# Between two expert mixtures: moving averages as banded products, and a new order of the stage

## The chip, the cores and the metric

The kernel runs on one core of a Trainium2 chip. The metric is the device time of one execution in microseconds; of several executions the median is given. All engines of the core work at the same time: PE (TensorE; PEld is its weight load), DVE (VectorE), ACT (ScalarE), POOL (GpSimd) and SP (SyncE, which here issues the weight transfers). Each works through its own instructions in order and waits at an instruction until what it needs is there. Results of PE go to PSUM, which the kernel divides into eight banks of 128 x 512 numbers of 32 bits; DVE and ACT take them from there.

## What is computed

A two-layer model over 512 tokens of width 1024. Layer 0 is attention, layer 1 averages over neighbouring tokens; each is followed by a mixture of 32 experts with two chosen per token. The stage at issue lies between the two mixtures:

```python
mod_l = (cond_lat @ w_ada[i] + b_ada[i])[:, None, :]
sh_m, sc_m, g_m, sh_f, sc_f, g_f = jnp.split(mod_l, 6, axis=-1)
h_l = modulate(rms_norm(x_lat, norm_mix_g[i]), sh_m, sc_m)       # h * (1 + scale) + shift
...
for gi, win in enumerate((2, 4, 8, 16)):                         # pool_mixer: 4 groups of 256 columns
    lo = jnp.maximum(t - win // 2, 0)
    hi = jnp.minimum(t + win // 2, n)
    mean = (cg[:, hi] - cg[:, lo]) / (hi - lo)                   # cg: running sum over the tokens
    outs.append((mean - h[..., sl]) @ w_pool[gi])
...
x_lat = x_lat + g_m * o_l
tokens = modulate(rms_norm(x_lat, norm_ffn_g[i]), sh_f, sc_f)
f = hierarchical_moe(tokens, ...)                                # group by argmax, then the two best experts
```

## The kernel before

All of x stays on chip as four tiles of 128 tokens by 1024 columns (`self.x(j)`, j = 0 to 3). Weights arrive as tiles of 1 MiB through one stream: `Stream` (L115) issues the loads on SP in a fixed order, at most 12 tiles are resident at a time, and `st.done()` after the last use of a tile lets the next load be issued. Tiles of this size, the weights among them, share 22 slots (`big`, L516).

**The mixture** (`moe`, L1547) runs 16 pairs of experts: up product, activation, down product, scatter back. The last pair of the first mixture is written out in `last_down` (L1416): the down product in two halves of the columns, `parted` (the gated rows, split into a high and a low part by DVE, ACT, DVE), `added` (scatter on PE, addition to x on DVE, squares on ACT), and then the norms `r` of the four token tiles. In the stream, eight tiles of `w_ada` follow the last expert of the first mixture, and behind them come the twelve tiles of the first pair of the second mixture. At the start of a mixture, `overflow` (L1479) makes every engine, SP too, read a count from DVE (`fullest`); only then does SP issue further loads.

**The stage between** (`pool_layer`, L1649) does this:
- `ada` (L1654): the modulation vectors of layer 1's mixture from `w_ada`, eight steps of four products each on PE (`ada_part`, L351); at the end `ada_rows` is copied by DVE, and `ada_end` (L432) turns the rows on PE and adds biases on DVE.
- `scaled` (L1638): x times its norm, token tiles 0 and 2 on DVE, 1 on ACT, 3 on POOL.
- `turned(k)` (L1663): for each of the eight column blocks k, four transposes on PE (tokens along the free axis), then scale and shift on ACT into a padded buffer.
- `sums(k)` (L1677): the moving sum by repeated doubling, one addition for a window of 2, up to four for a window of 16, and two small corrections at the edges; for k = 7, 5 and 3 on POOL, else on DVE. `less(k)` (L1691): mean minus input, on DVE. Group g consists of k = 2g and 2g + 1 and has the window 2, 4, 8 or 16.
- `project(g)` (L1698): eight products on PE; `added(g)` (L1712): addition to x on DVE and squares on ACT.
- `router` (L1120): 16 products on PE, then DVE scales the router weights. `turn(k)` (L1723) transposes x for the router, `logits` (L1732) are 16 products for four k. Norm (`rstd_of`), `norm_high` on ACT and `norm_low` on DVE make a high and a low part of the scaled tokens; `add_shift`, `choose` and `rank` on DVE choose the experts; `zeros` (L1323) clears four PSUM banks by a product of zeros; `gather_part` (L1329) gathers the tokens of the first eight experts by 64 products, and the second mixture begins.

The order on every engine is the order in which the program issues the instructions; there is no planner. It stands at the end of `pool_layer`: `turned` for 7, 0, 1, 6, 5; two ada steps; sums; `project(0)`, and so on, with `project(3)`, `project(2)`, `project(1)`, `ada_end` and `router` in this order.

Of the kernel before, what the change touches and what calls it, by code (L numbers as in the profile page):

```python
# [60 lines left out]

_C = {}
_off = 0
for _n, _w in (("ident", 128), ("iota", SEQ), ("tcol", NT), ("w8", EPG), ("w4", NG),
               ("islot", UNIT), ("edge", 4 * 16), ("tri", 128), ("cos", NT * HD), ("sin", NT * HD)):
    _C[_n] = (_off, _off + _w)
    _off += _w
# [3 lines left out]
def make_consts():  # L71
# [25 lines left out]
    sn = np.stack([-sn, sn], axis=-1).reshape(NT, 128, HD).transpose(1, 0, 2)  # L97
    put("cos", cs.reshape(128, -1))
# [84 lines left out]
class Kernel:  # L183
# [3 lines left out]
    def build(self):  # L187
        tc, nc, a = self.tc, self.nc, self.a
        with ExitStack() as es:
# [12 lines left out]
            with ExitStack() as sm:  # L202
# [7 lines left out]
                norms = self.moe(0, self.prepare_pool(), xe, later=later)  # L210
# [1112 lines left out]
    def zeros(self, k, tag):  # L1323
# [92 lines left out]
    def last_down(self, aT, w, gf, inv, after):  # L1416
# [38 lines left out]
        products(1, 1)  # L1455
        parted(1)
# [90 lines left out]
    def moe(self, i, late, first, then=lambda: None, later=iter(())):  # L1547
# [41 lines left out]
        for p in range(NPAIR):  # L1589
# [22 lines left out]
            if p == NPAIR - 1:  # L1612

                nc.scalar.activation(self.sm.tile([128, 1], F32, name="warm", bufs=1), self.rk[:, 0, 0:1], AF.Sqrt)
                return self.last_down(aT, w, gf, inv, then)
# [22 lines left out]
    def scaled(self, norms, outs):  # L1638

        nc = self.nc  # L1640
        engs = nc.vector, None, nc.vector, nc.gpsimd
        for j, r in norms:
            if engs[j] is None:
                nc.scalar.activation(outs[j], self.x(j), AF.Copy, scale=r)
            else:
                engs[j].tensor_scalar(outs[j], self.x(j), r, 0.0, op0=ALU.mult, op1=ALU.add)

    def pool_layer(self, norms):
        nc, mp, pm, st, sm, pw = self.nc, self.mp, self.pm, self.st, self.sm, self.pw  # L1649
        xn = [self.big([128, 2, D], F32, "xn") for _ in range(2)]  # L1650
        xnj = [xn[j // 2][:, j % 2] for j in range(NT)]
        self.ada_begin(pm, 1, 2, "ga")

        def ada(n):  # L1654
            for _ in range(4 * n):
                self.ada_part()

        ada(1)
        self.scaled(norms, xnj)
        PAD = 16  # L1660
        A, B = self.AB[1, 1, 0], self.AB[1, 0, 0]

        def turned(k):  # L1663

            ab = self.big([128, 3, SEQ + 2 * PAD], F32, "pab")
            h = ab[:, 0]
            nc.gpsimd.memset(h[:, :PAD], 0.0)
            nc.gpsimd.memset(h[:, PAD + SEQ:], 0.0)
            p = pm.tile([128, 512], F32, tag=("y", "c")[k // 2 % 2], name="pt")
            for j in range(NT):  # L1670
                nc.tensor.transpose(p[:, j * 128:(j + 1) * 128], xnj[j][:, k * 128:(k + 1) * 128], self.ident)
# [228 lines left out]
```

## Time and profile before

| | |
|---|---|
| time, median of 3 runs | 1384.36 us (1382.53 to 1388.68) |
| time of the profiled execution | 1387.86 us |
| its span | 1386.1 us |
| busy share of the span | PE 95%, DVE 48%, ACT 26%, POOL 11% |
| moved by DMA | 475.49 MB, mean 343 GB/s |

All times in the rows are microseconds from the start of the span. The first mixture ends at about 843, the stage between lasts until 911.5, the second mixture from there to 1362. In the page's forty slices, the moved GB/s are at 415 to 427 in both mixtures and fall to 130 and 266 in the two slices that hold the stage between. A busy PE is not a PE at its peak: a product is shown until its result is there, so the distance between starts is the price of one in a series.

### The profile page before, as it was taken

To read this page: it belongs to the slowest core of one execution; us is meant where nothing else is said; L and a number is where in the kernel's file an instruction comes from. 1 tells how busy PE (TensorE), PEld (TensorE's weight loads), DVE (VectorE), ACT (ScalarE), POOL (GpSimd) and SP (SyncE) were. 2 spreads that over 40 slices of the span, in tenths; PEclk is the share of its full clock that TensorE was granted. 3 is DMA by queue.
4 is the path that set the end of the run, shared out by engine and by line. 5 is a ranking of instruction groups with operands and counts; after the bars stand their busy time and mean duration, and the time that the engine had idled before them with its cause. 6 is when DMAs were issued, how large, how long until landed. Compare 5 with 4: busy or idle time off the path is not lost. (4 is left out here: it accounts for less than half of the span.)

```text
span 1386.1 us, 18610 instructions
## 1 busy us (share of the span) xinstructions
PE 1315.6 (95%) x7139; PEld 735.6 (53%) x7139; DVE 669.5 (48%) x1296; ACT 362.1 (26%) x703; POOL 146.4 (11%) x154
## 2 busy tenths in 40 slices
PE   4799999999899999999999997899999999999995
PEld 1578677778645444454444434654445444454442
DVE  2778788867824343343433437743334342343325
ACT  2554687763311111111111114421111111111103
POOL 1523343340000000000000014000000000000001
PEclk8799999999999999999999999999999999999998
DMA  9411836159489999999999999369999999999994
GB/s 374 166 62 61 342 143 215 52 187 389 191 368 427 427 427 426 426 427 426 427 426 427 422 417 416 130 266 396 427 427 426 427 426 427 426 426 427 426 421 172
DMA packets 80561, 475.49 MB, mean 343 GB/s; under 512 B 8497, under 2 KB 10049, under 8 KB 30289
## 3 DMA queue, kind: packets, MB, share of 16 engines
q1 hardware_dynamic: 80456, 474.22, 83.3%
q8 instruction: 58, 0.95, 0.3%
q14 instruction: 39, 0.31, 0.1%
q10 hardware_dynamic: 8, 0.01, 0.0%
HBM read 472.09 MB, written 2.11 MB: 342 GB/s over the span
## 5 line engine op out<-in xcount | busy, mean ns | idle before, releaser
L1356 PE MATMUL pgate<-wt,xe 128*64 128x512 f32 x1024 | 271.3, 593 | 2.8 <-ACTq L1488 2.2
L1356 PE MATMUL pup<-wt,xe 128*64 128x512 f32 x1024 | 270.2, 592 | 0.3 <-DVEq L1488 0.3
L1381 PE MATMUL py<-wt,aT 128*64 128x512 f32 x960 | 212.6, 595 | 0.0
L1361 DVE TENSOR_TENSOR act<-act,pup 128x512 f32<-128x512 f32 x32 | 22.0, 688 | 341.8 <-ACT act L1360 309.6
L1412 DVE TENSOR_TENSOR x<-x,pc 128x512 f32<-128x512 f32 x240 | 154.1, 684 | 29.8 <-PE pc L1410 29.8
L1356 PEld LDWEIGHTS pgate<-wt,xe 128*64 128x64 f32 x1024 | 75.6, 137 | 147.5 <-issue 129.8
L1356 PEld LDWEIGHTS pup<-wt,xe 128*64 128x64 f32 x1024 | 76.5, 137 | 145.2 <-issue 142.8
L1410 PE MATMUL pc<-y,scat 128*128 128x512 f32 x480 | 136.6, 406 | 2.4 <-DVE x L1412 2.4
L1394 DVE SCALAR_TENSOR_TENSOR py<-py,r_sw,gw 128x512 f32<-128x512 f32 x64 | 48.6, 759 | 178.4 <-PE py L1381 169.4
L1381 PEld LDWEIGHTS py<-wt,aT 128*64 128x64 f32 x960 | 66.9, 137 | 124.0 <-issue 118.8
L1311 PE MATMUL pga<-OH,xnp 128*128 128x224 f32 x896 | 119.3, 277 | 0.0
L1311 PEld LDWEIGHTS pga<-OH,xnp 128*128 128x128 f32 x896 | 114.3, 191 | 8.5 <-issue 1.6
L1360 ACT ACTIVATE act<-pgate 128x512 f32<-128x512 f32 x32 | 19.1, 598 | 359.7 <-PE pgate L1356 359.6
L1410 PEld LDWEIGHTS pc<-y,scat 128*128 128x128 f32 x480 | 80.3, 189 | 42.8 <-ACT act L1360 24.3
L1395 ACT ACTIVATE y<-py 128x512 fp32r<-128x512 f32 x64 | 38.3, 598 | 235.1 <-PE py L1381 160.0
L1320 POOL MEMSET xe<- 128x64 f32 x16 | 2.4, 152 | 783.7 <-PE pup L1356 556.4
L1345 ACT ACTIVATE xe<-pga,mod 128x224 f32<-128x224 f32 x64 | 34.0, 540 | 156.8 <-PE pga L1311 137.1
L548 PE MATMUL pmm<-whl,hT 128*128 128x512 f32 x288 | 70.3, 400 | 0.0
L836 DVE TENSOR_REDUCE mx<-S 128x1 f32<-128x768 f32 x64 | 58.3, 952 | 19.5 <-PE S L833 18.8
L548 PEld LDWEIGHTS pmm<-whl,hT 128*128 128x128 f32 x288 | 54.3, 192 | 11.3
L843 ACT ACTIVATE P<-S,mx 128x768 f32<-128x768 f32 x64 | 57.1, 901 | 2.2 <-POOL rest L717 2.0
L853 PE MATMUL PT<-cst,P 128*128 128x128 f32 x384 | 54.4, 277 | 0.1
(340 smaller groups left out, 1438.9 us busy)
## 6 DMA issues: line engine op xcount, KB each, us to landing
wt<-in_moe_w_gate_up_dram SPq DMA_DIRECT2D x224, 1024.0 KB
wt<-in_moe_w_down_dram SPq DMA_DIRECT2D x120, 1024.0 KB
wt<-in_w_ada_dram SPq DMA_DIRECT2D x48, 1024.0 KB
wt<-in_moe_w_gate_up_dram SPq DMA_DIRECT2D x64, 512.0 KB
wt<-in_moe_w_down_dram SPq DMA_DIRECT2D x16, 512.0 KB
wt<-in_attn_w_qkv_dram SPq DMA_DIRECT2D x6, 1024.0 KB
x<-in_x_dram SPq DMA_DIRECT2D x8, 512.0 KB
wt<-in_attn_w_o_dram SPq DMA_DIRECT2D x4, 1024.0 KB
```

The source lines that it names most:

```text
L548: self.nc.tensor.matmul(p, lhs(pa, k), whl[pb, k // 4][:, k % 4], start=(k + n == 0), stop=(k == KD - 1 and n == 2))
L836: nc.vector.tensor_reduce(m, s[:, :NKEY], axis=AX, op=ALU.max, negate=True)
L843: nc.scalar.activation(P[n][:, g], S.pop((n, g))[:, :NKEY], AF.Exp, bias=mx[n, g], accum_out=total[n // 4][:, 2 * gp + g, kvl:kvl + 1])
L853: nc.tensor.transpose(pt[:, cc, g * 128:(g + 1) * 128], P[n][:, g, c * 128:(c + 1) * 128], self.ident)
L1311: nc.tensor.matmul(p[:, :n], self.parts[part][j // 2][:, j % 2, k * 128:(k + 1) * 128], OH[:, j], start=(z == 0), stop=(z == 2 * NT - 1))
L1345: nc.scalar.activation(xe, p, AF.Identity, bias=B[:, k:k + 1], scale=A[:, k:k + 1])
L1356: nc.tensor.matmul(p[64 * e:64 * e + 64], xe(k)[:, offs[e]:offs[e] + UNIT], w[e][:, h * 512:(h + 1) * 512], start=(k == 0), stop=(k == KD ...
L1381: nc.tensor.matmul(py[h][64 * e:64 * e + 64], aT[:, j, 64 * e:64 * e + 64], wd[e][:, h * 512:(h + 1) * 512], start=(j == 0), stop=(j == 3) ...
L1394: nc.vector.scalar_tensor_tensor(py, py, w, gf[:, h * 512:(h + 1) * 512], op0=ALU.mult, op1=ALU.mult)
L1395: nc.scalar.activation(y[:, 0], py, AF.Copy)
L1410: nc.tensor.matmul(p, P[:, j * 128:(j + 1) * 128], y[:, part], start=(part == 0), stop=(part == 1))
L1412: nc.vector.tensor_add(xs, xs, p)
```

## The change

The averages over 8 and 16 tokens (groups 2 and 3, k = 4 to 7) are computed by PE: the scaled tokens, not yet transposed, are multiplied by a band matrix that holds 1/(number of tokens) inside the window. A band reaches from one token tile into its neighbours, so four products with 131 to 143 columns are added up in one bank, on top of one product of zeros that clears it; then ACT scales and shifts the result as it does the input itself, and one subtraction on DVE is left. The bands (three shapes for each of the two windows, 812 columns of 128 numbers) are new constants and are loaded by a DMA that ACT's queue issues (`pool_begin`). Nothing but four small memsets of margins and the memset of `xe` is left to POOL; token tile 3 is scaled on ACT.

The eight ada steps move: two into `last_down` between the last down product and `parted(1)`, four ahead of the transposes, two after the first means. `ada_end` stands behind `project(0)` and two groups of transposes, the router's products and the zeros for the logits behind `project(3)`, ahead of `summed(2)`. Transposes for the router come earlier or on other engines, all four `low` steps of token tiles 0 and 1 stand ahead of `add_shift`, and each of the four banks of the gather is cleared by three products of zeros in place of one.

```diff
@@ constants
+BANDS = {}
+for _w in (8, 16):
+    BANDS[_w, 0], BANDS[_w, 1], BANDS[_w, 2] = 128 + _w // 2, 127 + _w, 127 + _w // 2
@@ def zeros(self, k, tag, n=1):
-        self.nc.tensor.matmul(p, self.tri_b[:, 0:1].to_broadcast([128, 128]), self.ones_b[:, 0:1].to_broadcast([128, 512]), start=True,
-                              stop=False)
+        for z in range(n):
+            self.nc.tensor.matmul(p, ..., start=(z == 0), stop=False)
@@ def last_down(self, aT, w, gf, inv, after, gap):
         after()
         products(1, 1)
+        gap()
         parted(1)
@@ def scaled(self, norms, outs):
-        engs = nc.vector, None, nc.vector, nc.gpsimd
         for j, r in norms:
-            if engs[j] is None:
+            if j % 2:
                 nc.scalar.activation(outs[j], self.x(j), AF.Copy, scale=r)
...
+    def pool_begin(self):
+        self.bands = self.mp.tile([128, NT, 4 * CAP], F32R, name="OH").rearrange("p a b -> p (a b)").bitcast(F32)
+        a, b = _C["band"]
+        self.nc.scalar.dma_start(self.bands[:, :b - a], self.a["consts"][:, a:b])
+        self.ada_begin(self.pm, 1, 2, "ga")
+        self.ada_parts(2)
@@ def pool_layer(self, norms):
+        self.ada_parts(4)
...
+        def means(k, tag):
+            g, w = k // 2, WINDOWS[k // 2]
+            p = pm.tile([128, 512], F32, tag=tag, name="pm")
+            nc.tensor.matmul(p, *zero, start=True, stop=False)
+            for j in range(NT):
+                t0, t1 = max(0, 128 * j - w // 2 + 1), min(SEQ, 128 * j + 128 + w // 2)
+                o = offs[w, 0 if j == 0 else 2 if j == NT - 1 else 1]
+                nc.tensor.matmul(p[:, t0:t1], xnj[j][:, k * 128:(k + 1) * 128], self.bands[:, o:o + t1 - t0], start=False,
+                                 stop=(j == NT - 1))
+            modulated(k, hm[g][:, k % 2, 1], p)
+        def less(k):
+            h, m = (hm[k // 2][:, k % 2, z] for z in range(2))
+            nc.vector.tensor_tensor(h, m, h, op=ALU.subtract)
+            diff[k] = h
...
-        (the order before: turned 7, 0, 1, 6, 5; ada; sums; ... project 0, 3, 2, 1; ada_end; router)
+        for js in (range(2), range(2, NT)):
+            for k in (0, 1, 6, 7):
+                turned(k, js)
+        padded(0); padded(1); plain(6); plain(7)
+        summed(0); means(6, "g"); means(7, "u"); summed(1)
+        self.ada_parts(2)
+        turned(4); turned(5); less(6); less(7); plain(4); plain(5)
+        means(4, "g"); means(5, "u")
+        p0 = project(0, ("t", "y"))
+        turned(2); turned(3)
+        self.ada_end("y")
+        less(4); less(5); padded(2); padded(3)
+        added(*p0)
+        p3 = project(3, ("g", "u"))
+        self.router(1, self.gw[:, 1])
+        self.norm_begin()
+        nc.tensor.matmul(self.lg, *zero, start=True, stop=False)
+        summed(2); summed(3)
+        p2 = project(2, ("t", "y"))
+        added(*p3)
+        turn(0, "c", nc.scalar); turn(1, "c", nc.scalar)
+        p1 = project(1, ("g", "u"))
+        added(*p2)
+        turn(6, "y", nc.scalar); turn(7, "c", nc.vector)
+        added(*p1)
+        turn(4, "y", nc.vector); turn(5, "c", nc.vector)
         logits(0, 1, 6, 7)
@@ after the norm
-        high(0); turn 2 and 3; low(0, 0); logits(4, 5, 2, 3); high(1); low(0, 1); low(1, 0)
+        turn 2 and 3; high(0); high(1); logits(4, 5, 2, 3); low(0, 0); low(0, 1); low(1, 0); low(1, 1)
...
-            self.zeros(k, tag)
-        low(1, 1)
+            self.zeros(k, tag, 3)
```

`padded(k)` is the old way into a padded buffer for k = 0 to 3, `plain(k)` the scaled and shifted input without margins for k = 4 to 7, `summed(k)` the old doubling on DVE together with its subtraction. Several calls are written on one line here.

## Rows read from the trace of the kernel before

**Rows 1.** Windows: stretch, length; busy us (instructions) by engine; granted clock, DMA share, GB/s
```profile
844.00:850.50 6.50, 4.90 (x20) 3.95 (x20) 2.97 (x11) 3.68 (x5) 1.95 (x9) 0.58 1.01 417
850.50:865.00 14.50, 13.39 (x81) 8.28 (x84) 12.65 (x17) 4.47 (x12) 12.01 (x18) 0.95 1.02 415
865.00:878.70 13.70, 11.70 (x60) 7.91 (x61) 10.96 (x18) 5.84 (x19) 2.81 (x6) 0.88 0.88 359
878.70:892.70 14.00, 14.00 (x131) 13.58 (x130) 7.42 (x21) 6.39 (x14) 0.15 (x1) 1.00 0.01 2
...
900.20:911.50 11.30, 10.37 (x64) 10.19 (x64) 5.66 (x14) 1.92 (x5) 0.00 (x0) 0.72 0.01 3
911.50:1362.00 450.50, 448.31 (x2276) 212.56 (x2278) 164.97 (x299) 56.61 (x96) 1.06 (x7) 1.00 1.00 420
```
**Rows 2.** Timeline of SP's queue: start, length, engine line operation, tensors, count
```profile
820.16 9.33 SPq L122 DMA_DIRECT2D wt<-in_w_ada_dram  x8
...
864.26 2.98 SPq L122 DMA_DIRECT2D wt<-in_moe_w_down_dram  x4
912.36 12.58 SPq L122 DMA_DIRECT2D wt<-in_moe_w_gate_up_dram  x8
```
**Rows 3.** Timeline, entry to the stage; in brackets idle time before and its releaser
```profile
836.98 0.58 ACT L1395 ACTIVATE y<-py 128x512 fp32r<-128x512 f32 x1
...
843.50 1.15 ACT L1644 ACTIVATE xn<-x,nr 128x1024 f32<-128x1024 f32 x1
...
844.10 0.33 PE L1671 MATMUL pt<-cst,xn 128*128 128x128 f32 x1 [3.38 <-DVE xn L1646]
...
845.11 1.58 POOL L1646 TENSOR_SCALAR xn<-x,nr 128x1024 f32<-128x1024 f32 x1 [43.48 <-PE pt L1671]
```
**Rows 4.** Timeline, PE series at the full clock
```profile
853.04 3.72 PE L1705 MATMUL pp<-pw,pab 128*128 128x256 f32 x16
...
857.57 1.92 PE L357 MATMUL ada_ps<-wt,cond 128*32 128x512 f32 x16
...
880.02 1.95 PE L1127 MATMUL pb<-gw,mod 128*128 128x128 f32 x16
...
882.71 1.91 PE L1729 MATMUL pb<-cst,x 128*128 128x128 f32 x16
...
884.46 3.74 PE L1736 MATMUL pb<-gw,xT 128*128 128x128 f32 x32
...
894.20 1.03 PE L1326 MATMUL pga<-ones_b,tri_b 128*128 128x512 bf16 x4
```
**Rows 5.** Timeline, DVE additions beside POOL's and alone
```profile
864.65 3.02 DVE L1685 TENSOR_TENSOR pab<-pab 128x541 f32<-128x541 f32 x2
...
870.42 0.72 DVE L1681 TENSOR_TENSOR pab<-pab 128x543 f32<-128x543 f32 x1
...
872.21 1.29 DVE L1695 SCALAR_TENSOR_TENSOR pab<-pab 128x512 f32<-128x512 f32 x2
```
**Rows 6.** Timeline: end of the logits' wait, and the gather
```profile
892.68 0.74 DVE L1167 SCALAR_TENSOR_TENSOR L<-pb,n4r,bw 128x36 f32<-128x36 f32 x4 [1.04 <-PE pb L1736]
...
900.25 10.37 PE L1334 MATMUL pga<-OH,xnp 128*128 128x224 f32 x64 [0.16 <-DVE OH L1537]
```
**Rows 7.** Groups by form, 830 to 913: busy us, mean ns of one
```profile
L1156 DVE SCALAR_TENSOR_TENSOR xnp<-x,n4r,xnp 128x512 fp32r<-128x512 f32 x8 | 5.7, 748 | 0.2 <-ACT xnp L1152 0.2
```
**Rows 8.** Timeline, far from the stage: transposes, ada products, a transfer of ACT's queue
```profile
12.33 3.65 PE L630 MATMUL ph<-cst,xn 128*128 128x128 f32 x16 [4.34 <-DVE xn L608]
15.91 3.64 PE L357 MATMUL ada_ps<-wt,cond 128*32 128x512 f32 x32
...
377.32 2.24 ACTq L264 DMA_DIRECT2D gates<-in_b_ada_dram  x2
...
383.23 1.27 POOL L440 TENSOR_TENSOR gates<-gates,ada_rows 64x512 f32<-64x512 f32 x1 [23.73 <-DMA gates<-in_b_ada_dram]
```
**Rows 9.** Chain that ended last: a gather of the second mixture at the full clock
```profile
928.00 2.88 PE pga L1311 x24
```

More of the change, by code (lines that the diff above doesn't have):

```diff
@@ L97, in make_consts @@
     sn = np.stack([-sn, sn], axis=-1).reshape(NT, 128, HD).transpose(1, 0, 2)
+    bands = []
+    for w, z in BANDS:
+        tile = (0, 1, NT - 1)[z]
+        src = 128 * tile + np.arange(128)[:, None]
+        t = max(0, 128 * tile - w // 2 + 1) + np.arange(BANDS[w, z])[None]
+        lo, hi = np.maximum(t - w // 2, 0), np.minimum(t + w // 2, SEQ)
+        bands.append(((src >= lo) & (src < hi)) * (np.float32(1) / (hi - lo).astype(np.float32)))
+    put("band", np.concatenate(bands, axis=1))
     put("cos", cs.reshape(128, -1))
@@ L1545, in one_hot, with moe @@
         return OH
-    def moe(self, i, late, first, then=lambda: None, later=iter(())):
+    def moe(self, i, late, first, then=lambda: None, later=iter(()), gap=lambda: None):
         nc, st = self.nc, self.st
@@ L1737, in logits @@
                                      start=False, stop=(k == 3 and j == NT - 1))
-        ab = {}
-        for k in (7, 0, 1, 6, 5):
-            ab[k] = turned(k)
-        ada(2)
-        sums(7, ab[7], nc.gpsimd)
-        sums(5, ab[5], nc.gpsimd)
-        for k in (0, 1):
-            sums(k, ab[k], nc.vector)
-            less(k, ab.pop(k))
-        p0 = project(0)
-        for k in (4, 3):
-            ab[k] = turned(k)
-        ada(2)
-        sums(3, ab[3], nc.gpsimd)
-        sums(6, ab[6], nc.vector)
@@ L1754, in pool_layer @@
-        less(6, ab.pop(6))
-        less(7, ab.pop(7))
-        added(*p0)
-        p3 = project(3)
-        ab[2] = turned(2)
-        ada(2)
-        sums(4, ab[4], nc.vector)
-        less(4, ab.pop(4))
-        less(5, ab.pop(5))
+        for js in (range(2), range(2, NT)):
+            for k in (0, 1, 6, 7):
+                turned(k, js)
+        padded(0)
+        padded(1)
+        plain(6)
+        plain(7)
+        summed(0)
+        means(6, "g")
+        means(7, "u")
+        summed(1)
@@ new lines, in pool_layer @@
+        self.ada_parts(2)
+        turned(4)
+        turned(5)
+        less(6)
+        less(7)
+        plain(4)
+        plain(5)
+        means(4, "g")
+        means(5, "u")
+        p0 = project(0, ("t", "y"))
+        turned(2)
+        turned(3)
+        self.ada_end("y")
+        less(4)
+        less(5)
+        padded(2)
+        padded(3)
+        added(*p0)
+        p3 = project(3, ("g", "u"))
+        self.router(1, self.gw[:, 1])
+        self.norm_begin()
+        nc.tensor.matmul(self.lg, *zero, start=True, stop=False)
@@ L1763, in pool_layer @@
+        summed(2)
+        summed(3)
+        p2 = project(2, ("t", "y"))
         added(*p3)
-        p2 = project(2)
-        sums(2, ab[2], nc.vector)
-        less(2, ab.pop(2))
-        less(3, ab.pop(3))
         turn(0, "c", nc.scalar)
         turn(1, "c", nc.scalar)
+        p1 = project(1, ("g", "u"))
         added(*p2)
-        ada(1)
-        p1 = project(1)
-        self.ada_end("c")
+        turn(6, "y", nc.scalar)
+        turn(7, "c", nc.vector)
         added(*p1)
-        self.router(1, self.gw[:, 1])
@@ L1776, in pool_layer @@
[L1776 to L1780 removed]
         turn(4, "y", nc.vector)
[L1782 removed]
+        turn(5, "c", nc.vector)
         logits(0, 1, 6, 7)
@@ L1793, in low @@
             self.norm_low(j, r[:, j:j + 1], *hl[j], k)
-        high(0)
         turn(2, "y", nc.vector)
         turn(3, "c", nc.scalar)
+        high(0)
+        high(1)
+        logits(4, 5, 2, 3)
         low(0, 0)
-        logits(4, 5, 2, 3)
-        high(1)
         low(0, 1)
         low(1, 0)
+        low(1, 1)
         self.route_begin()
```

77 lines of the change are left out of this document (42 added, 35 removed).

## The prediction

> **What bounds the kernel now.** First the windows over the end of the trace [rows 1]. From 911.5 to 1362 the second mixture runs at 420 GB/s with a DMA share of 1.00 and PE busy almost throughout: nothing that happens before changes its length. What counts is when it starts. The transfers stand still from 878.7 (share 0.01, then 0.01 again up to 911.5), because SP has issued its last load at 864.26 and the next only at 912.36 [rows 2], when the count of the chosen experts is there. So the weights of the first pair lie on chip 30 us before they are used, and a microsecond taken out between 843 and 911.5 comes out of the total, whole, as long as that margin lasts. (That the profiled execution took 1387.86 us and the median is 1384.36 lies in runs, not in the stage; I subtract the gain from the median.)
>
> Next, within the stage, the windows again [rows 1]. From 844 to 850.5 PE has 4.90 busy of 6.50 at a granted clock of 0.58: it waits for the scaled tokens and then works mostly at 1.2 GHz. From 850.5 to 865 POOL (12.01 of 14.5), DVE (12.65) and PE (13.39) are all full, and they hinder one another: two additions of 541 columns on DVE take 3.02 beside POOL's, 1.5 each, while one of 543 alone takes 0.72 [rows 5]. From 865 to 878.7 PE waits for DVE's differences and loses clock (0.88). From 878.7 on PE is the bound, until the choice on DVE, and the gather runs at 0.72 of the clock.
>
> **The change, part by part.** I follow the path engine by engine, in times of the trace of before.
>
> *Entry.* The two ada steps in the gap cost PE 2 x 0.85 = 1.7 (0.85 each: 32 records, four steps, in 3.64 and 16 in 1.92 [rows 4, 8]). They lie between the last down product and the scatter, which waits for ACT's pass at 836.98, so for 837.56. One DVE pass of 0.75 [rows 7] lies between that product and ACT's pass; the product is there by 836.2, the two steps end by 837.9 at the latest. Bounds 0 and 0.3, taken 0, since ACT's pass may have waited for ACT itself. Four more take 3.4 from about 839.7 on (PE idle 3.38 before 844.10, one ada step ahead of that [rows 3]), in the wait for the scaled tokens: covered if their weights are there. Behind them 12.6 MB of the first pair are queued, and the windows move 2.7, 6.0 and 4.9 MB from 844 to 878.7 [rows 1]: so the last `w_ada` tile lands near 846.6 and the others 2.45 earlier each, the sixth near 841.6. The bands' 0.42 MB push that to about 842.6; its products are done by 843.5. Margin 0.6 us. The DMA issue itself stands on ACT ahead of the row at 836.98. Two issues of ACT took 2.24 [rows 8], SP's 1.17 and 0.75 each [rows 2]; ACT may work off earlier squares meanwhile. Bounds 0 and 1.1 on the path, taken 0.2: the two issues of ACT are small transfers like this one, but nothing waited behind them that would show a cost.
>
> *Scaled tokens.* Token tile 3 goes from POOL (845.11, 1.58, so 846.69) to ACT, free from 844.65, at 1.15 [rows 3]: ready at 846.2, with the 0.2 at 846.4. By then the transposes of tiles 0 to 1 are out; seven or eight at 0.11 (16 in 1.91 [rows 4]) are left and end at 847.2.
>
> *PE's series, 847.2 on.* A banded product has 131 to 143 columns; the nearest row is 128 columns at 0.114 per record, two records each, hence about 0.24 [rows 4]; four of them and a product of zeros at 0.22 make 1.18 per k. Upper bound: each at the price of 256 columns, 0.445 [rows 4], so 2.0 per k and 3.3 more in all. Four k: 4.7. Two ada steps 1.7, 16 transposes 1.8, `project(0)` and `project(3)` at 3.56 each 7.1 [rows 4], `ada_end`'s four transposes 0.45, the router 1.9 and its 16 small products 0.6. Sum 18.2, so the router's result is there at about 865.5. Is PE fed? DVE needs two windows of 2 (each the 2.44 below less one addition, some 1.7, from 847.6 to 851), then the copy of the ada rows and two subtractions of about 0.65: done by 854, and `project(0)` needs only the first two. ACT has ten passes of 512 columns, below 1 us each (1024 took 1.15 [rows 3]). Yes.
>
> *DVE's queue gets two new waits.* Its `ada_end` additions wait for transposes that stand behind `project(0)` on PE, until about 859.5; behind them on DVE stand `less(4)`, `less(5)` and the addition of group 0, and `project(2)` and the router's bank wait for those, without loss (862.5). Then the router's copies wait for PE until 865.5, and behind them stand `summed(2)` and `summed(3)`, for which `project(1)` waits. That is the handover: 0.65 for the router's copies, 2 x 2.44 for the sums (870.42 to 872.86 for one, with two subtractions in 1.29 [rows 5]), and half of `added(3)`, which frees the bank: 871.8. No doubling of DVE's additions any more, since POOL adds nothing. PE does `project(2)` and two turns meanwhile and then rests some 2 us.
>
> *Second series.* From 871.8: `project(1)` 3.56, four turns 1.75, logits 3.6, two turns 0.9, logits 3.6 [rows 4] = 13.4, result at 885.3. `low` four times at 0.75 [rows 7], for which ACT makes the `high` parts after its copy of the turned block (882.5; two passes of 1.2): the second pair of `low` starts about 885 and ends at 886.4, now 1 us behind the logits, which were last before [rows 6]. So `add_shift` begins at 886.4 where it began at 892.68 [rows 6]: **6.3 earlier**.
>
> *From there to the gather* the same steps follow, one `low` fewer ahead of `rank` (0.1): the gather starts at about 893.9 where it started at 900.25 [rows 6]. The eight added products of zeros (0.216 each, 1.7) fall into the 5.0 us from the old ones' end at 895.2 to the gather [rows 4, 6], in which PE waits for DVE's choice: free.
>
> *The gather's clock.* 64 products took 10.37 [rows 6] at a granted 0.72 [rows 1]; at the full clock, 24 take 2.88 [rows 9], so 64 take 7.7. With them, and the logits now 1 us ahead of DVE, PE's rest before the gather becomes 4.2 where it was 5.0. Bounds 0 and 2.7; from 865 to 878.7 PE rested only 2.0 us (11.70 of 13.70) and lost clock (0.88 [rows 1]), so I expect that 4.2 us cost it too, and take 0.4.
>
> Sum: 6.3 + 0.1 + 0.4 = 6.8 against the profiled execution. Its clock was low in three stretches of the stage; the last covered most of the gather, which a typical execution need not have, so I take 0.4 off: 6.4. **1384.4 - 6.4 = 1378.0 us.**
>
> **The rivals.**
>
> *PE's clock falls in the new first series.* What PE does from 844.3 to 847.2 is transposes with pauses; the stretch 844 to 850.5 was at 0.58 before [rows 1]. A fall at this place, as long as that one, costs half of 6 us of a series in which PE is now the bound: 3.0, so 1381.0. Against it: ada products now fill the wait that preceded that fall, and at the start of the kernel 16 transposes alone ran at half clock (3.65, 0.22 apart), after which the ada products directly behind them ran at 0.85 a step, the full clock [rows 4, 8]. The Trainium skill (TensorE: Matmul & The Clock Gate, Part 4: PE-mode transpose) says that transposes do not count as PE being busy for the clock in the same way; by that rule the fall would happen and 1381 be right. The row of the sixteen transposes speaks against the rule, if not beyond doubt. Chance 0.17.
>
> *The bands come late.* They are issued near 836.4 and needed at 847.2. If they had to wait behind all weights already issued, as the last `w_ada` tile did (issued by 829.5 [rows 2], landed near 846.6, 17 us), they would land at 853.5, and PE with everything behind would stand for 6.3: 1384.3. Against it: a transfer of ACT's queue issued at 377.32 to 379.6 was used at 383.23 [rows 8], 6 us at most, in a stream of weights. The Trainium skill (DMA: Bandwidth & Descriptors, Issuing engines are not separate DMA queues) says that transfers of different engines run on the same 16 DMA engines and interleave; so the bands would share and not queue, and the trace agrees. Chance 0.07.
>
> *The gather at the full clock* (the third zeros do their work): 2.7 for 0.4, so 1375.7. For it: less rest; against it: 4.2 us of rest is twice what went with a fall from 865 on. Chance 0.18.
>
> *Slower:* DVE's and PE's queues now hand over to each other, PE, DVE, PE, and each pause may take the clock. PE is the bound for 18.2 + 13.4 = 31.6 us of the stage. At 1.2 GHz throughout this would add 31.6 and give 1409.6. The point from which it decides: 13 us of these at half clock (cost 6.4) bring no change, 26 us bring a loss of over 0.5%. Before, the stage had about 10 us at half clock. Chance 0.05.
>
> That the banded products do not relieve anything is excluded by POOL: its 12 us leave in any case.
>
> **How the numbers follow.** Forecast 1378.0, chance 0.53, with its own range 1375.5 to 1381 (bounds of the issue +0.9, of the gap's products +0.3, of the banded products +3.3, of the gather, and a microsecond each way of the medians). Rivals 0.17, 0.07, 0.18, 0.05. The range over all: down to 1373.5 (full clock in the gather, issue free, runs a little fast), up to 1384.5 (late bands, or a fall of the clock with dear banded products); it leaves out about 0.15. A measurement here can tell 0.5%, 6.9 us, from no change: the bound is 1377.4, just under the forecast. So the forecast itself gives 0.24 faster and 0.29 within; the full-clock gather 0.16 and 0.02; the clock rival and the late bands are within; of the slower case 0.04 is beyond the bound. Faster 0.40, within 0.56, slower 0.04.
>
> **What would show it.** Right: in the stage's middle POOL close to idle, no DVE addition of 540 columns above 0.8; ada products directly ahead of the transposes and no PE wait for weights; DVE waiting for PE twice, some 5 and 3 us, ahead of the second addition of `mod` and of the router's copies; `add_shift` near 886; SP's first load of the second mixture about 6 to 7 earlier than 912.36. Wrong: a PE wait for the bands at the first mean; the granted clock below 0.9 between 850 and 865; banded products over 0.3 apart; a wait of ACT for slots or memsets; a second mixture that grows by what the stage gave.

## The result and the profile after

The kernel after takes 1393.49 us (median, 1391.08 to 1396.04) beside 1384.64 for the kernel before on the same chip: the ratio is 1.006 (95% interval 1.0045 to 1.0074). So it is slower by 8.9 us, where 6.4 us less were forecast. Its profiled execution spans 1393.4 us. One execution of e9 below took 2697.79 us, twice the others, and is left out of its median.

The windows over the stage in the trace of after, beside [rows 1]: stretch, length, busy us (instructions) of PE, PEld, DVE, ACT and POOL, granted clock, DMA share, GB/s.

```profile
840.50:852.17 11.67, 0.67 (x8) 0.00 (x0) 0.00 (x0) 0.00 (x1) 0.00 (x0) 0.73 1.01 422
852.17:861.82 9.65, 8.39 (x40) 3.56 (x41) 5.81 (x20) 4.84 (x13) 0.80 (x4) 0.62 1.02 418
861.82:879.40 17.58, 17.53 (x123) 14.78 (x121) 9.26 (x19) 10.57 (x17) 0.32 (x4) 1.00 1.00 392
...
910.19:920.11 9.92, 9.08 (x65) 8.89 (x65) 5.48 (x14) 1.87 (x4) 0.00 (x0) 0.83 0.02 4
920.11:1370.00 449.89, 447.67 (x2276) 212.68 (x2278) 164.90 (x299) 56.57 (x96) 1.06 (x7) 1.00 1.00 420
```

In the first line, 11.67 us long, no engine computes anything but PE, which finishes an ada step, while the transfers run at 422 GB/s. That is the loss, and it lies at the stage's entry. The third line is the new first series of PE: 17.53 busy of 17.58 at the full clock, POOL at 0.32 where it had 12.01 of 14.5 (eight memsets of margins are left to it in the whole stage, not four). The gather takes 9.92 to the first product of the second mixture where it took 11.3, and the second mixture runs as before.

Who stands, the timeline of the same kernel says (start, duration, engine, line, operation; in brackets idle time before and its releaser); it answers [rows 3]:

```profile
840.32 0.19 ACT L1460 ACTIVATION_READ_ACCUMULATOR act<-x 128x1 f32 x1
852.17 0.36 ACTq L1672 DMA_DIRECT2D OH<-in_consts_dram  x1
852.78 0.60 ACT L1410 ACTIVATE y<-py 128x512 fp32r<-128x512 f32 x1 [12.28 <-DMA wt<-in_moe_w_gate_up_dram]
853.43 3.78 PE L1456 MATMUL pc<-y,scat 128*128 128x512 f32 x8 [12.26 <-ACT y L1410]
...
864.04 1.12 PE L1742 MATMUL pm<-OH,xn 128*128 128x136 f32 x8
```

ACT ends its last square at 840.5 and starts nothing until 852.17, when it issues the load of the bands (L1672). Its pass for the second half of the mixture's last rows (L1410) comes 0.6 behind that; PE's scatter waits 12.26 for the pass, and all that follows waits for the scatter. The bands themselves are not late: they are wanted at 864.04 and had landed by 858.46.

What does the issue wait for? Not for its tile: e3, below, fills the same tile from 801.05 on. The trace's record of the issue names semaphore 101 (a semaphore is a counter; a transfer raises its own as its pieces land): the issue waits until it has been raised far enough. The transfers of SP and ACT take eight semaphores in turn (101 to 104, 106 to 109), and the one that had 101 before was the last tile of `w_ada`, issued by SP at 832.58; its last piece landed at 852.15, 0.02 us ahead of ACT's issue. (The brackets name a `gate_up` tile instead: whose landing ended a wait is inferred by the profile, and the semaphores' own times are the better source.) SP, too, stands at its issues for landings; its waits in the trace of after (engine, line, what for: us in total, times, longest):

```profile
SPq L136 <- DMA wt<-in_moe_w_gate_up_dram: 182.8, 131, 3.3
SPq L136 <- DMA wt<-in_moe_w_down_dram: 115.4, 69, 3.1
```

For SP, which does nothing else, that is a limit on how far it runs ahead. For ACT it is a stop of the whole stage.

The rest of the change did what was forecast. The timeline of after from the middle of the stage on, answering [rows 4 to 6]:

```profile
871.30 3.62 PE L1759 MATMUL pp<-pw,pab 128*128 128x256 f32 x16
...
876.26 0.17 DVE L472 TENSOR_TENSOR mod<-pb,cols 128x8 f32<-128x8 f32 x1 [5.40 <-PE pb L458]
...
882.09 0.17 DVE L1150 COPY mod<-pb 128x16 f32<-128x16 f32 x1 [3.03 <-PE pb L1147]
...
888.27 3.69 PE L1759 MATMUL pp<-pw,pab 128*128 128x256 f32 x16 [1.58 <-DVE x L1771]
...
902.62 0.74 DVE L1181 SCALAR_TENSOR_TENSOR L<-pb,n4r,bw 128x36 f32<-128x36 f32 x4
903.50 2.57 PE L1341 MATMUL pga<-ones_b,tri_b 128*128 128x512 bf16 x11
...
910.19 9.08 PE L1349 MATMUL pga<-OH,xnp 128*128 128x224 f32 x64 [0.27 <-DVE OH L1553]
```

DVE's two new waits (5.40 and 3.03), PE's rest ahead of the last projection (1.58) and the shift added to the logits without idle time ahead of it are all there. The shift follows the scatter's start by 902.62 - 853.43 = 49.2 us; before it was 892.68 less 837.61 (the scatter's start, 0.63 behind the row at 836.98 [rows 3]), so 55.1 [rows 6].

The sum, profile against profile: the scatter starts 15.8 later. Of that, 12.3 are ACT's wait, and 3.4 are the first mixture's end: its last pair's activation on ACT came at 823.39 in after and at 819.97 in before. The stage behind the scatter is 7.3 shorter (66.7 against 73.9 to the first product of the second mixture), so the second mixture starts 8.6 later; the two spans differ by 7.3. The first mixture's 3.4 are not of the change, which begins behind it: 0.6 are there from the first pair on and 2.8 come in the last three pairs, and in e8, the same program up to the gap, the last three pairs took as long as in before within 0.2. That activation of the last pair lies between 817.6 and 821.2 in the traces of all twelve experiments; 823.39 is the exception.

### The profile page after: what moved, and what is told of

Same layout as the page of the kernel before. It is cut to its first block, busy times and chain, and to the rows that moved or that the text cites. A ratio compares the mean times of both kernels' runs of the same rounds, so it can differ in the third digit from the quotient of the medians.

```text
span 1393.4 us, 18658 instructions
## 1 busy us (share of the span) xinstructions
PE 1318.3 (95%) x7179; PEld 738.4 (53%) x7183; DVE 659.7 (47%) x1290; ACT 364.1 (26%) x707; POOL 130.8 (9%) x130
## 5 line engine op out<-in xcount | busy, mean ns | idle before, releaser
L1396 PEld LDWEIGHTS py<-wt,aT 128*64 128x64 f32 x960 | 66.9, 137 | 124.0 <-issue 118.8
L1410 ACT ACTIVATE y<-py 128x512 fp32r<-128x512 f32 x64 | 38.2, 597 | 247.4 <-PE py L1396 182.0
L562 PEld LDWEIGHTS pmm<-whl,hT 128*128 128x128 f32 x288 | 54.3, 192 | 11.3
```

The source lines that it names most:

```text
L562: self.nc.tensor.matmul(p, lhs(pa, k), whl[pb, k // 4][:, k % 4], start=(k + n == 0), stop=(k == KD - 1 and n == 2))
L1396: nc.tensor.matmul(py[h][64 * e:64 * e + 64], aT[:, j, 64 * e:64 * e + 64], wd[e][:, h * 512:(h + 1) * 512], start=(j == 0), stop=(j == 3) ...
L1410: nc.scalar.activation(y[:, 0], py, AF.Copy)
```

## The experiments

"Stage" is the time from the scatter's start to the first product of the second mixture in the profiled execution.

| kernel | median us | ratio to before (95%) | scatter starts | stage |
|---|---|---|---|---|
| before | 1384.6 to 1385.4 | 1 | 837.6 | 73.9 |
| after | 1393.49 | 1.006 (1.0045 to 1.0074) | 853.4 | 66.7 |
| e1 bands early, on SP | 1380.16 | 0.9958 (0.9942 to 0.9973) | 837.8 | 66.3 |
| e2 before, with the load | 1398.63 | 1.0096 (1.0074 to 1.0118) | 848.3 | 71.8 |
| e3 load on POOL | 1379.39 | 0.9954 (0.9939 to 0.9968) | 838.1 | 65.6 |
| e4 before, wide table | 1384.02 | 0.9988 (0.9977 to 0.9999) | 836.3 | 70.9 |
| e5 = e1, one zero | 1380.90 | 0.9969 (0.9956 to 0.9983) | 837.0 | 70.4 |
| e6 = e1, five zeros | 1379.06 | 0.9958 (0.9942 to 0.9974) | 837.8 | 66.8 |
| e7 = e1, router behind | 1380.02 | 0.9959 (0.9945 to 0.9973) | 838.9 | 67.0 |
| e8 = after, four small loads | 1393.02 | 1.0057 (1.0042 to 1.0073) | 848.0 | 67.4 |
| e9 = after, load on SP | 1393.00 | 1.0057 (1.0038 to 1.0075) | 836.9 | 80.8 |
| e10 = e1, load among `w_ada` | 1379.24 | 0.9955 (0.9941 to 0.9969) | 837.8 | 66.9 |
| e11 = e10, e7 and e6 | 1375.99 | 0.9932 (0.9919 to 0.9946) | 838.6 | 62.2 |
| e12 = after, four pieces | 1398.67 | 1.0093 (1.0075 to 1.0110) | 857.1 | 68.1 |

### The load and the rest, apart: e1 and e2

e1, against after: the three lines of the load leave `pool_begin` and stand, on SP, behind the `yield` in `prepare_pool`.

```diff
         yield
+        self.bands = self.mp.tile([128, NT, 4 * CAP], F32R, name="OH").rearrange("p a b -> p (a b)").bitcast(F32)
+        a, b = _C["band"]
+        nc.sync.dma_start(self.bands[:, :b - a], self.a["consts"][:, a:b])
...
     def pool_begin(self):
-        self.bands = self.mp.tile([128, NT, 4 * CAP], F32R, name="OH").rearrange("p a b -> p (a b)").bitcast(F32)
-        a, b = _C["band"]
-        self.nc.scalar.dma_start(self.bands[:, :b - a], self.a["consts"][:, a:b])
         self.ada_begin(self.pm, 1, 2, "ga")
```

> The kernel after, with the load of the band constants moved: SP issues it during the last but one pair of the first mixture, and ACT issues no transfer in the gap. Theory A (ACT, which works in order, stood at the issue of this load from 840.5 to 852.17 us because the issue waited for an older weight transfer to land, and everything behind it stood too, 12.28 us): the y row on ACT follows the squares at about 841 us without idle time of that size, and the time falls by 12.3 us to about 1381, or to 1382 if the 416 KB of the load (1.0 us at the 414 GB/s of that stretch) delay the last weights of the mixture. If the 3.4 us by which the first mixture ended later were of the load or of chance, it falls further, to about 1378. Theory B (the new order of TensorE's work is what costs, and ACT's idle time only hides it): ACT's idle time goes, but the waits turn up in the series behind it, and the time stays within 3 us of 1393.5.

e2, against before: the table of constants with the bands, and in the gap of `last_down` the same load on ACT. Nothing reads it.

```diff
         products(1, 1)
+        self.bands_load()
         parted(1)
```

> The kernel before with nothing but the load of the band constants, which it doesn't use, issued by ACT at the place where the kernel after issues it. Theory A (the issue holds ACT until an older weight transfer has landed): ACT idles about 12 us ahead of its y row, and the time rises by 10 to 12.5 us to 1395 to 1397. Theory B (the new order costs, not the load): the time stays within 1.5 us of 1384.6. If the wider table of constants or the 416 KB slow the first mixture by 3.4 us, that comes on top: its last pair ends later by that much.

The four kernels make a square. After was timed beside another set of runs of before (1384.64) than e1 and e2 (1385.36), so each is set against its own: e1 gains 5.2, after loses 8.9, e2 loses 13.3. The load costs before 13.3 us (10 to 12.5 were expected), and it costs after 8.9 + 5.2 = 14.1 us. The rest of the change gains 5.2 without the load and 13.3 - 8.9 = 4.4 with it. Each interval is some 2 us wide either way, so the two pairs agree. In e2, where PE's order is that of before, ACT stands as in after:

```profile
847.14 0.36 ACTq L1665 DMA_DIRECT2D OH<-in_consts_dram  x1
847.68 0.60 ACT L1407 ACTIVATE y<-py 128x512 fp32r<-128x512 f32 x1 [12.32 <-DMA wt<-in_moe_w_gate_up_dram]
```

and the piece for which it waits landed at 847.12, again 0.02 us ahead. In e1 the pass follows its squares at once, and the stage is as short as in after. Its timeline:

```profile
837.06 0.57 ACT L1410 ACTIVATE y<-py 128x512 fp32r<-128x512 f32 x1
...
844.94 1.06 PE L371 MATMUL ada_ps<-wt,cond 128*32 128x512 f32 x8 [1.38 <-DMA wt<-in_w_ada_dram]
...
845.94 1.97 PE L1700 MATMUL pt<-cst,xn 128*128 128x128 f32 x16
...
847.96 1.12 PE L1742 MATMUL pm<-OH,xn 128*128 128x136 f32 x8
...
866.01 0.18 DVE L1150 COPY mod<-pb 128x16 f32<-128x16 f32 x1 [3.02 <-PE pb L1147]
...
872.20 3.69 PE L1759 MATMUL pp<-pw,pab 128*128 128x256 f32 x16 [1.58 <-DVE x L1771]
...
886.55 0.74 DVE L1181 SCALAR_TENSOR_TENSOR L<-pb,n4r,bw 128x36 f32<-128x36 f32 x4
...
894.12 9.09 PE L1349 MATMUL pga<-OH,xnp 128*128 128x224 f32 x64 [0.27 <-DVE OH L1553]
```

Theory B, that the new order itself costs, falls with this pair. That the load costs 13.3 to 14.1 where ACT stands 12.3 has one part to be seen: during the wait the granted clock falls, the scatter behind it takes 3.78 for its eight products, and the stage is 0.4 longer in after than in e1. The rest is within the scatter of the runs.

### Which engine issues it, and where: e3 and e9

```diff
-        self.nc.scalar.dma_start(self.bands[:, :b - a], self.a["consts"][:, a:b])
+        self.nc.gpsimd.dma_start(self.bands[:, :b - a], self.a["consts"][:, a:b])    # e3
+        self.nc.sync.dma_start(self.bands[:, :b - a], self.a["consts"][:, a:b])      # e9
```

> The kernel after, with the same load at the same place of the program, but issued by GpSimd instead of ACT. Theory A (ACT's order is what stood still): ACT runs on, the scatter of the last half starts near 841 us, and what remains is whether the bands land ahead of the first banded product; if they land by 855 us the time is about 1381, and if GpSimd's issue is held as ACT's was, to 852, the products wait some 3 to 5 us and it is 1384 to 1387. Theory C (it is the arrival of the bands that costs, whoever issues them): the time stays within 2 us of 1393.5, with the wait ahead of the banded products in place of that ahead of the y row.

> The kernel after, with the load at its place in the program but issued by SP instead of ACT. ACT then waits for nothing, as in e1 and e3, but SP, which also works in order, comes to the load only behind seven weight tiles, at 852 us or later, and the bands land behind these tiles. Theory A (an engine in order stands where the issue stands, and the bands' arrival is a second, separate condition): ACT's y row starts near 837 us, the first banded product, which stood at 847.96 in e1, waits until about 860, and the time is 12 us above e1's 1380.2, so near 1392. Theory C (arrival costs nothing, since other work of TensorE fills the time): 1381 to 1383.

The same line of the program on another engine runs at another time. From the timeline of e3:

```profile
801.05 0.72 POOL L1672 DMA_DIRECT2D OH<-in_consts_dram  x1
...
837.39 0.58 ACT L1410 ACTIVATE y<-py 128x512 fp32r<-128x512 f32 x1
```

POOL has little work in the mixture and comes to the load 36 us ahead of the place where ACT does; its transfer takes another semaphore (116) and landed at 807.96. So the bands landed early, and e3 says only that the stop is ACT's, not what late bands cost. e9 says that:

```profile
836.20 0.57 ACT L1410 ACTIVATE y<-py 128x512 fp32r<-128x512 f32 x1
...
850.16 0.33 SPq L1672 DMA_DIRECT2D OH<-in_consts_dram  x1
...
859.91 2.23 PE L1742 MATMUL pm<-OH,xn 128*128 128x136 f32 x8 [12.65 <-DMA OH<-in_consts_dram]
```

ACT runs on, but SP comes to the load at 850.16, the bands land at 859.86, and PE waits 12.65 for them: 1393.00. Two conditions stand one behind the other, ACT's order and the bands' arrival, and at this place of the program each alone costs some 13 us. An issue that runs earlier meets both: on POOL, which comes to it at 801.05 (e3), or on SP further ahead in the program (e1, and e10 below).

### The 3.4 us of the first mixture: e4

The kernel before with the wider table alone (the entry `band` in `_C` and its columns).

> The kernel before with only the table of constants wider by the 812 columns of the bands; nothing loads them. It asks whether the 3.4 us by which the first mixture ended later in the trace of the kernel after belong to the table. If they are chance of one profiled execution: 1384.6 within 1 us. If the wider rows of the table or the other addresses of the inputs slow the transfers: about 1388, with the last pairs of the first mixture later by about 3 us.

It takes 1384.02, ratio 0.9988: the table is free. The last pair's activation came 1.3 earlier than in the trace of before, as did the pairs ahead of it (1.1 to 1.4). So e4 and e8 put the 3.4 down to one execution. Its stage, 70.9, and e2's 71.8 show something else: the trace on which the prediction rests, with 73.9, shows a long stage.

### What the issue waits for: e8 and e12

e8 puts four loads of 64 bytes on SP's queue ahead of ACT's load; e12 cuts ACT's load into four.

```diff
+        for z in range(4):                                                   # e8
+            self.nc.sync.dma_start(self.sm.tile([1, 16], F32, name=f"small{z}", bufs=1), self.a["consts"][0:1, :16])
...
-        self.nc.scalar.dma_start(self.bands[:, :b - a], self.a["consts"][:, a:b])
+        for z in range(0, b - a, 203):                                       # e12
+            self.nc.scalar.dma_start(self.bands[:, z:z + 203], self.a["consts"][:, a + z:a + z + 203])
```

> The kernel after, with four loads of 64 bytes on SP's queue put into the program just ahead of ACT's load of the bands; nothing uses them. It asks what the issue waits for. Theory A (the transfers of all queues take eight semaphores in turn by their order in the program, and each issue waits until the transfer before it on its semaphore has landed): four places further on, the load's semaphore is 106 instead of 101, the transfer before it is the one that landed at 858.06 us in the trace of after instead of 852.15, ACT's idle time grows from 12.28 to about 18.2 us and the time rises by 5.9 to about 1399.4. Theory B (the issue waits for its tile, for the queue of ACT or for the weights in general): ACT issues at 852 us as before, within 0.5 us, and the time stays at 1393.5. The trace also shows whether the first mixture, the same here as in after, again ends 2 to 3 us later than in before, or whether that was chance.

The forecast of 1399.4 was wrong: 1393.02. The timeline of e8:

```profile
846.68 0.36 ACTq L1674 DMA_DIRECT2D OH<-in_consts_dram  x1
847.30 0.60 ACT L1410 ACTIVATE y<-py 128x512 fp32r<-128x512 f32 x1 [12.64 <-DMA wt<-in_moe_w_gate_up_dram]
...
849.12 4.97 SPq L1673 DMA_DIRECT2D small<-in_consts_dram  x4
```

The small loads, written ahead of ACT's, took the semaphores behind it (103, 104, 106, 107), and ACT's kept 101: the turn isn't the source's order over two engines. So e8 changed nothing of the wait. It still ended 0.02 us behind a landing (846.66), but the test told no theory from the other, and e12 was made in its place, with four issues on one engine.

> The kernel after, with ACT's load of the bands at the same place cut into four of 203 columns each. In e8 the four small loads of SP came behind ACT's load in the turn of the semaphores (103, 104, 106 and 107; the load kept 101), so the turn is not that of the source and e8 left the wait as it was. Four loads on one engine must take four places of the turn. Theory A (each issue waits until the transfer before it on its semaphore has landed; in the traces of after, e8 and e2 the issue followed that landing by 0.02 us): the pieces take 101, 102, 103 and 104 and the fourth waits for a landing 3.75 us after the first's (855.92 against 852.15 in after), so ACT idles about 16 us ahead of its y row instead of 12.28, and the time rises by 3.7 to about 1397. Theory B (ACT waits once, for its tile, its queue or the transfers in flight): the three further issues cost 0.36 us each, ACT idles about 13.4 us and the time is 1394.6.

```profile
850.60 5.62 ACTq L1673 DMA_DIRECT2D OH<-in_consts_dram  x4
856.42 0.60 ACT L1410 ACTIVATE y<-py 128x512 fp32r<-128x512 f32 x1 [18.83 <-DMA OH<-in_consts_dram]
```

The pieces took 101, 102, 103 and 106, a weight tile of SP 104. They were issued at 850.60, 851.83, 853.04 and 855.89; the transfers before them on these semaphores had landed at 850.58, 851.81, 853.02 and 855.87. Four issues, four landings, 0.02 us each. The time rose to 1398.67, 5.2 above after or, each against its own runs of before, 4.5; that is more than the 3.7 expected because the fourth piece took 106 and not 104. One wait for the tile or the queue would have cost 1.1.

### The smaller prices: e5, e6, e7, e10 and e11

e5 and e6 change `self.zeros(k, tag, 3)` of e1 to 1 and 5. e7 moves the router:

```diff
         p3 = project(3, ("g", "u"))
-        self.router(1, self.gw[:, 1])
-        self.norm_begin()
-        nc.tensor.matmul(self.lg, *zero, start=True, stop=False)
         summed(2)
         summed(3)
         p2 = project(2, ("t", "y"))
         added(*p3)
+        self.router(1, self.gw[:, 1])
+        self.norm_begin()
+        nc.tensor.matmul(self.lg, *zero, start=True, stop=False)
```

> The kernel of e1_bands_early with one product of zeros for each bank during the choice, as before the change, instead of three. It prices that part of the change. In e1 the granted clock is at half for 3.41 us from 894.91, 0.8 us after the gather's start, and the gather takes 9.09 us; in the three profiled kernels with one zero for each bank the gather took 10.37, 9.28 and 9.07 us. Theory A (the zeros shorten the half clock): the gather takes 9.3 to 10.4 us and the time rises by 0.2 to 1.3 us over e1's 1380.16. Theory B (three zeros are too few or too early to matter): the gather takes 9.1 us and the time stays within 0.3 us.

> The kernel of e1_bands_early with five products of zeros for each bank instead of three: twenty of 0.234 us each (2.57 us for 11 in e1), which end near 892.1 us, ahead of the ranking's products at 892.82. Theory A (TensorE's idle 2.8 us ahead of the ranking is what lowers the clock in the gather): the half clock goes, the gather takes 64 x 0.12 = 7.7 us instead of 9.09, and the time falls by 1.4 us to 1378.8. Theory B (the half clock comes from other idle time, or the zeros don't count): the gather stays at 9.1 us and the time within 0.3 us of 1380.2.

> The kernel of e1_bands_early with the router's products and copies put behind the running sums of window 4 and the sums into x of the fourth group, so that VectorE does not wait 3.02 us for the router's products at 866.01. Theory A (this wait lies on the path to the projection of the second group, which starts at 872.20 after an idle 1.58 us of TensorE): VectorE's sums end 3 us earlier, the projection starts at about 870.9 behind the router's products, and the time falls by 1.3 us to 1378.9. Theory B (TensorE's own order bounds this stretch): no more than 0.3 us.

The three medians lie within 1.1 us of e1's, and their intervals overlap: no price is settled by the times. The traces say more for the router. From the first transpose to the shift took 40.6 us in e1, e3, e6 and e10 alike and 39.3 in e7, the 1.3 expected; the projection follows DVE without a rest:

```profile
872.28 0.17 DVE L1150 COPY mod<-pb 128x16 f32<-128x16 f32 x1 [0.48 <-PE pb L1147]
...
873.27 3.62 PE L1759 MATMUL pp<-pw,pab 128*128 128x256 f32 x16
```

But e7's transposes began 1.1 later behind the scatter in that execution, and the gather ran 0.9 longer, at half clock from 893.78 for 6.8 us. For the zeros, the gather took 9.88 in e5 with one, 9.09 in e1 with three and in e6 with five, but 9.99 in e7 with three: the place where the clock falls varies by more than the zeros move it. The half clock that e6 was to remove is still there in its gather (3.4 us from 895.82).

e10 lets SP load the bands between the sixth and seventh tile of `w_ada`:

```diff
             self.ready.append((key, t))
             self.out += 1
+            self.behind.pop(key, lambda: None)()
...
+        self.st.behind[("ada", 1, 2, 5)] = load
```

> The kernel of e1_bands_early with SP's load of the bands moved from ahead of the last down weights of the mixture to between the sixth and the seventh of the eight tiles of w_ada. In e1 the load's 406 KB stand ahead of weights that the mixture waits for: its last pair ended 0.8 us later against the pairs before it than in before, and TensorE waited 1.67 and 2.29 us for the fifth and sixth tiles of w_ada, so that the transposes began 8.19 us behind the scatter's start against 6.49. Theory A (these transfers bound the entry): the mixture ends 0.8 us earlier, the transposes begin some 7.5 us behind the scatter's start, and the time falls by 1 to 1.5 us to about 1379; the bands land near 846 and the last tile of w_ada near 851, 0.7 us after its step is wanted, which ACT's pass ahead of the next transposes hides. Theory B (the differences are chance of one execution): within 0.3 us of 1380.2.

> The kernel of e10 with the router put behind as in e7 and five products of zeros as in e6. If the gains add (1 to 1.5 us of e10, 1.1 us of e7, by the stretch from the scatter to the lowest products without its half clock, and 0 to 1 us of the zeros) the time is about 1377; if the half clock at the entry or in the gather falls differently, 1376 to 1381.

e10's 1379.24 is 0.9 below e1, which the spread doesn't tell from nothing; the transposes began 7.76 behind the scatter for e1's 8.19. e11 takes 1375.99 (1375.42 to 1376.71), the fastest here: 0.9932 of before. In its trace PE does not rest from 873 us to the last zeros, and, alone of all these traces, it has the full clock from the scatter through the gather:

```profile
884.88 0.74 DVE L1183 SCALAR_TENSOR_TENSOR L<-pb,n4r,bw 128x36 f32<-128x36 f32 x4
885.56 4.54 PE L1343 MATMUL pga<-ones_b,tri_b 128*128 128x512 bf16 x20
...
892.45 7.46 PE L1351 MATMUL pga<-OH,xnp 128*128 128x224 f32 x64 [0.27 <-DVE OH L1555]
```

Of the 4.1 us that its stage is shorter than e1's, 1.6 are the gather (7.46 for 9.09), 1.6 the way from the first transpose to the shift (39.0 for 40.6), and 0.9 the earlier transposes. Why the clock held here and not in e6, with the same zeros and the same 1.0 us of rest behind them, isn't settled: e6 has one more rest, 1.6 us ahead of the projection, 20 us earlier.

## Why the prediction was wrong

**The step that failed** is in the part *Entry*: "The DMA issue itself stands on ACT ahead of the row at 836.98 ... Bounds 0 and 1.1 on the path, taken 0.2". Measured: 12.28 us. The bounds came from the wrong thing. I divided the length of a group of issues by their count ([rows 2, 8]) and called it the price of an issue; but one issue of SP takes 0.33 us here and ACT's took 0.33 to 0.36, and the rest of SP's 1.17 is a wait for landings. The trace of before shows this wait, and the prediction draws nothing from it:

```profile
SPq L122 <- DMA wt<-in_moe_w_gate_up_dram: 174.5, 124, 2.6
SPq L122 <- DMA wt<-in_moe_w_down_dram: 113.1, 67, 2.2
```

The two issues of ACT in [rows 8], 1.71 and 0.49 long and the only ones of ACT in that trace, could not show it: they took semaphores 107 and 108, and the transfers before them on these had landed at 346.50 and 348.93, 30 us earlier. Put on ACT, the same wait lasts as long as the transfer that it meets: 20 us from issue to landing at this place, since `w_ada` tile 8 was issued at 832.58 and landed at 852.15. I had worked out that latency myself (17 us, for the rival of the late bands) and asked it of the bands' arrival, not of the engine that issues them. No rival had ACT standing (among the signs of being wrong is a wait of ACT, but for slots or memsets), so the range, 1373.5 to 1384.5, could not hold the result.

**The two ada steps in the gap** cost nothing, as taken: in e1 the scatter starts 0.69 behind ACT's pass, 0.63 before.

**Four ada steps covered, with the sixth tile at 842.6 and 0.6 to spare:** wrong in size. In e1 the sixth step starts when its tile lands, at 844.94, and the transposes begin at 845.94. The banded products then start at 847.96 instead of 847.2: 0.8 lost. About half of that may be the load's own place in e1: in e10, where it stands behind the sixth tile, the sixth step starts at 844.52 and the banded products at 847.54. The rest is the reckoning itself: in the trace of before the sixth and the last tile of `w_ada` landed at 844.00 and 848.88, not near 841.6 and 846.6. After can't show it, since there all tiles landed during ACT's wait.

**PE's first series:** from the first banded product to the router's result 866.01 - 847.96 = 18.05, and 0.2 more with the zeros ahead of it, forecast 18.2; a mean with its four products and zeros follows the one before by 1.13 to 1.17, forecast 1.18, and the upper bound of 2.0 had no ground.

**DVE's waits, handover, second series:** 5.40 and 3.02, forecast some 5 and 3. The projection of the second group starts at 872.20 (forecast 871.8), the shift at 886.55 (886.4), the gather at 894.12 (893.9), all in e1.

**The gather's clock:** 9.09 for 10.37, so 1.3 gained where I took 0.4 of bounds 0 and 2.7. But not all of it is the change's: in e4 and e2, with one zero, the gather took 9.28 and 9.07.

**The typical execution:** I took 0.4 off because the profiled stage of before had low clock. Its stage of 73.9 is 2.1 to 3.0 above those of e2 and e4. Against these two, one execution each, the term was too small by some 2 us, which would explain why the rest of the change brings 5.2 where I forecast 6.4. It isn't shown: by e1's interval the gain is 3.7 to 8.0, so the times don't tell 5.2 from 6.4. With the load elsewhere the time is 1380.16, inside the range.

**The rivals.** *The clock falls in the first series:* not in after, e1, e3, e6, e10 and e11; in the executions of e5 and e7 that were profiled it was at half for 6.8 and 3.4 us from 844 to 851. It happens, now and then; in e5 the way from the first transpose to the shift took 42.7 for 40.6. The evidence that I set against it was weaker than it reads: that the sixteen transposes of [rows 8] ran at half clock is taken from their spacing of 0.22 alone, and the granted clock of their window (12.2 to 15.6) stands at 1.00 in the trace. So that row speaks neither for nor against the rule cited there, and no run here tests transposes alone. *The bands come late:* e9 made it true, at 13 us instead of 6.3, because an issue on SP is itself held up first. My evidence against it, a transfer of ACT's queue that took 6 us [rows 8], was right for the transfer (in after 852.17 to 858.46) and silent on the wait ahead of it, as its semaphores were free. The rule cited there from the Trainium skill (DMA: Bandwidth & Descriptors, Issuing engines are not separate DMA queues) speaks of transfers on their way, and these did interleave with the weights; it says nothing of a wait ahead of the issue. *The gather at the full clock:* in e11 alone. *Half clock throughout:* did not occur; PE's first series ran at 1.00 in after, e1 and e10. (The "about 10 us at half clock" given there for the stage before leaves out the gather: by [rows 1] it is 10.2 ahead of the gather and 6.3 in it.)

## What to carry to other kernels

Before a load is put on an engine that computes, look in the trace at what the issues of the other queues wait for: if they wait for landings, the new issue may have to wait too, for as long as transfers take at that place, and everything behind it on its engine with it. Give such a load to an engine that has nothing else to do, at a place in the program that lies ahead of its use by more than the latency and the issues queued there. And price an issue by one that stands in the same traffic: the length of a series mixes issuing with waiting, and an issue where the queues had just been idle shows no wait at all.

## What the runs showed of the hardware

SP's and ACT's transfers shared eight semaphores in turn, and an issue started 0.02 us after the last piece of the transfer before it on its semaphore had landed (after, e2, e8, and four times in e12); POOL's one load had another semaphore (e3) and did not wait for them. The wait is part of the issue as the trace records it, and the kernel's text does not name it; whether a program can be built without it, no run shows. A transfer of 406 KB landed 6.3 us after its issue in the midst of the weights (after), while a weight tile of 1 MiB took 20 us.

The granted clock differs from execution to execution: over e5's ten executions its mean went from 0.988, in the fastest (1377.19 us), to 0.982, in the slowest (1384.60). Between the last half of the first mixture's rows and the second mixture it was at half for 0 (e11) to 17.1 us (before) in the traces in which no engine stood for the load, and for 17.1 (after, e9) to 27.3 us (e12) in those in which one did; the same 64 products of the gather took from 7.46 (e11) to 10.47 us (e12). With one trace of each kernel, how much of that is the kernel's and how much the execution's is not told apart.
